# Two-layer streaming encoder trunk on one core: token tiles in another order, layer-norm scale and bias applied at the transposed copy, pooling loads ahead of the reloads, all gate units in the attention filler

## The chip, the cores and the metric

The kernel runs on one core of one Trainium2 chip. The metric is the device time of one execution in microseconds (us). The kernel before takes 2465.11 us, the median of three runs (2463.23 to 2467.07).

## What is computed

Two request groups, 1024 prompt tokens and 8 x 16 sample tokens, go through the same two layers of width 1024. The kernel treats them as T = 1152 tokens in nine tiles of 128; tile 8 is the sample group. The reference, cut to what matters:

```python
x = layer_norm(x, ln_in_g, ln_in_b)                      # entry
for each layer:
    h = x @ w_in -> px | pg | q | k | v | ag | ga | gb   # 512 | 512 | 5 x 1024 | 1024
    ya = pool_mix(px, history)  * silu(pg)               # 4 channel groups, windows 2, 4, 8, 16, each times w_pool[g]
    q, k = rope(q), rope(k)
    o  = diff_attend(q, k, v)                            # A1 - lambda * A2, RMS sub-norm per head
    yb = o * silu(ag)
    merged = sigmoid(ga) * (ya @ w_a) + sigmoid(gb) * (yb @ w_b)
    x = layer_norm(ALPHA * x + merged @ w_o, ln_g, ln_b)
```

All is fp32. Outputs are x of both groups and, for each layer, k, v and the last 15 rows of px.

## The kernel before

**Products.** A matrix product is made of three float32r products of a high and a low part: `xh` is a rounded copy of x (ScalarE), `xl` the rest (VectorE), and the same for weights (`wh`, `wl`, or `fa`, `fb` for some pieces). x is kept transposed, channels on partitions, for all nine token tiles.

**Weights.** Class `Weights` (L156 to L276) walks a fixed plan. `load` issues the DMA of the next piece into one of two staging tiles `ws`; `fill` splits staged pieces into hi (ScalarE, L243 or L257) and lo (VectorE, L244 or L258) as far as buffers are free; `get` hands a piece to its user and `free` gives its buffer back and fills again. For paired pieces `add` makes the four sums s1 to s4 (L195 to L198).

**Queues.** All DMAs are issued by SyncE (SP), in the order of the program. A DMA that waits (for its source to be written, or for its destination to be free) holds every DMA behind it. `later(n, fn)` puts an action off by n calls of `tick()`.

**Stages of a layer:**

1. *Entry (first layer) and first half of v.* A token tile's layer norm is statistics on VectorE (L374), `rs` and `nm` on GpSimd (L321, L326), two activations of 128x512 on ScalarE (L330), then gamma on VectorE (L335) and beta on GpSimd (L336). `to_T` (L300) transposes the finished tile on TensorE, copies it out of PSUM once as `xh` (L309) and once as fp32 `xs` (L312), with `xl` in between on VectorE (L310), and stores `xs` to the DRAM tensor `xT_d` (L313). The loop at L506 runs the nine tiles of v (`v_tile`, 24 matmuls of 128x512, L296 to L298); after each comes one step of `entry_rest` (L418): affine of one tile, norm of the next, transposition of an earlier one. gamma and beta are spread to 128 partitions by matmuls with a row of ones (L389). In the second layer the norm and affine steps belong to the end of the first, and only three transpositions remain for the loop.
2. *Operands of the seven-product scheme.* The rest of `x @ w_in` that is done at this point (q, k, px, pg, and ga) is computed in 16 pairs of 256 columns by a Strassen-like scheme: seven products e1 to e7 for each half c of the columns within the two token halves. The token half is HT = 576, a half of it CW = 288. For each c, `x_loads` reads four blocks of `xT_d` into `f` tiles (L471), `x_sums` makes t1 to t4 of them on VectorE (L477 to L480, 128x1152 each), and `x_split` makes hi and lo (L488, L489). t1 is written over a quadrant of `xh` and `xl`, which is saved in `b12_d` before (L513) and read back after the stage (L704). Products e1 and e2 use x itself and are the only ones that don't need t1 to t4. In the loop at L506 the loads for c = 0 come after tile 5 (first layer) or 3, those for c = 1 after tile 7 or 5, fixed in `l0, s0, l1, s1`.
3. *Lead.* In the first layer one attention-gate unit (72 matmuls, L528 to L541) stands between v and the products; LEAD = (1, 0).
4. *Products.* L555 to L698: the list `order` holds the products of all pairs, with the last product e7 of a column half held back by one; each result is joined on VectorE (L632) and leaves through rotation, tanh or a copy. After each finished operand `W.fill` is put off by one tick.
5. *Second half of v, with pooling.* L700 to L815. After the `b12_d` reload and small constants, the generator `pooling` loads two groups of px (`u_load`, L756 to L758), the gate values `sg` (L763) and the group's weights `wpl` (L765). It makes the window sums (`win_sums`), stores the history (`o_hp`, `o_hs`, L781 and L782) and forms the difference `pl` (`pool_diff`). `pool_mm` (L742) multiplies by `wpl` in three products of 128x384 (six rows of the trace), and writes `yah` and `yal`. One step of it follows each v tile: sums of group 0, product of group 0, sums of group 1, product of group 1, and so on. The loads of the next `sg` and `wpl` follow each product. `u` has two buffers: the loads of group 2 wait for the `o_hs` store of group 0.
6. *w_a*, then *attention* with two fillers: `filler` puts gate units (L882 and on) and w_b between the attention's matmuls, so that TensorE has work while softmax runs elsewhere. Then *w_o* with the layer norm (L1395 to L1470).

Of the kernel before, what the change touches and what calls it, by code (L numbers as in the profile page):

```python
# [17 lines left out]
P = 128  # L18
# [13 lines left out]
LEAD = (1, 0)  # L32
# [11 lines left out]

STEPS = [(1, 3), (2, 1), (4, 2), (3, 2), (3, 3), (1, 3, 4), (3, 5), (5, 5), (3, 5)]
# [11 lines left out]
def trunk(ctx, tc, a):  # L57
# [51 lines left out]
    cfix = const.tile([P, 4, 16], F32, name="cfix")  # L109

# [44 lines left out]
    class Weights:  # L155


        OPS = ("a11", "a12", "s1", "s2", "s4", "s3", "a22")

        def __init__(self):  # L160
# [13 lines left out]
            self.sums = None  # L174
            self.added = -1

        def load(self):
            while self.nload < len(self.loads) and self.held < NS:
# [8 lines left out]
                if e[0] == "p" and len(self.staged[i]) == 2 and self.sums is not None:  # L187
                    later(4, lambda i=i: self.add(i))

        def add(self, i):  # L190
            if self.added >= i:
                return
            self.added = i
            e1, e2 = self.staged[i]
            (sa, sb) = self.sums  # L195
            a11, a12, a21, a22 = e1[:, :512], e1[:, 512:], e2[:, :512], e2[:, 512:]
            s1, s2, s3, s4 = sa[:, :512], sa[:, 512:], sb[:, :512], sb[:, 512:]
            V.tensor_tensor(out=s1, in0=a21, in1=a22, op=ALU.add)  # L198
            V.tensor_tensor(out=s2, in0=s1, in1=a11, op=ALU.subtract)
            V.tensor_tensor(out=s4, in0=a12, in1=s2, op=ALU.subtract)  # L200
            V.tensor_tensor(out=s3, in0=a11, in1=a21, op=ALU.subtract)
# [18 lines left out]
        def fill(self, upto=1 << 30):  # L220
            while self.nsplit < min(len(self.items), upto):
                i, op = self.items[self.nsplit]
                tags = self.tags(op)
                if tags is None or (op is not None and op[0] == "s" and self.sums is None):
                    break
# [3 lines left out]
                if op is None:  # L229
# [8 lines left out]
                    else:  # L238
                        o = 4 * int(tags[0][1])
                        hi, lo = (x[:, o:o + 4, 2 * GW:2 * GW + 256] for x in (xh, xl))  # L240
# [5 lines left out]
                else:  # L246
                    if op[0] == "s":
                        self.add(i)
# [51 lines left out]
    def to_T(xn, t, pool, dst, one=None):  # L300
        two = None if one else ps_two()
        for b in range(2):
            ps = one() if one else two[:, b, :]
# [54 lines left out]
    gt = ep.tile([P, D], F32, name="gt")  # L358
    bt = ep.tile([P, D], F32, name="bt")
    dma(gt[0:1, :], a["ln_in_g"])  # L360
    dma(bt[0:1, :], a["ln_in_b"])
    for t in range(3):
        e_load(t)
    ones = ep.tile([1, P], F32, name="ones")
    G.memset(ones, 1.0)
    W.load()
    for t in range(3, 6):
        e_load(t)
# [15 lines left out]
    def spread(dst):  # L384
        out = []
        for b in range(2):
            ps = ps_any()
            c = slice(b * 512, (b + 1) * 512)
            PE.matmul(ps, ones, dst[0:1, c], start=True, stop=True)  # L389
            out.append((dst[:, c], ps))  # L390
        return out

    gps, bps = spread(gt), spread(bt)
    for dst, ps in gps:
        S.copy(dst, ps)
    e_norm(0)
    for dst, ps in bps:
        S.copy(dst, ps)
    e_norm(1)
    e_affine(0)  # L400
    e_norm(2)
    e_affine(1)
    e_turn(0)
    tick()
    e_affine(2)
    W.fill(1)
    W.fill(2)
    W.load()
    e_turn(1)
# [4 lines left out]
    e_turn(2)  # L414
    tick()
    for t in range(6, NT):
        e_load(t)

    def entry_rest():
        for n in range(3, NT + 2):  # L420
            if 3 <= n - 1 < NT:
                e_affine(n - 1)
# [1172 lines left out]
```

## Time and profile before

| what | value |
|---|---|
| median of three runs | 2465.11 us |
| profiled execution | 2470.53 us |
| its span | 2468.8 us |
| mean granted TensorE clock | 0.98 |
| TensorE busy | 2329.7 us, 94% |
| VectorE, ScalarE, GpSimd busy | 61%, 38%, 21% |

The stages lie as follows in the profiled execution, by the first matmul of each: first half of v from 25.4 us, lead unit from 98.4, products from 118.5, second half of v with pooling from 448.7, w_a from 519, attention from 575.7, w_o from 1153.8; second layer: v from 1257.0, products from 1316.0, pooling from 1646.8, w_a from 1721, attention from 1777.2, w_o from 2360.7.

To read it: a granted clock of 1.00 is TensorE at full speed, 0.50 at half. In a row of the waits, an engine's idle time is put down to what ended it. TensorE's rows have modelled ends, and matmuls overlap, so the time of one is not its pitch; the pitch is the difference of two starts.

### The profile page before, as it was taken

The page shows a single profiled execution, that of the slowest core. Times are in us where ns is not written, and L with a number is a line of the kernel's source. Part 1 is how long each engine was busy: PE and PEld are TensorE (multiplying, and loading weights), DVE is VectorE, ACT ScalarE, POOL GpSimd, SP SyncE. Part 2 cuts the span into 40 slices and gives each one's busy share as a digit, 9 for nine tenths or more (in the row PEclk, how much of TensorE's full clock was granted, in tenths as well). Part 3 has the DMA queues.
Part 4 walks back from the last instruction along what each step waited for, and adds up shares of the span by engine and source line. Part 5 has one row for each costly group of instructions (what it writes and reads, how often), then busy time and mean ns, then how long its engine had stood idle before and what let it go on. Part 6 is the DMA issues. An engine that isn't in the chain of part 4 may idle for free.

```text
span 2468.8 us, 40176 instructions
## 1 busy us (share of the span) xinstructions
PE 2329.7 (94%) x14936; PEld 2171.4 (88%) x14936; DVE 1510.9 (61%) x2903; ACT 932.7 (38%) x2054; POOL 519.0 (21%) x426
## 2 busy tenths in 40 slices
PE   7799999898999999999997999989899999999998
PEld 5689999687899998899877999987889898999986
DVE  5488854445677667744637886535467667666355
ACT  4332233212555555521433223332155555554122
POOL 4123300000121212232320332000012122213333
PEclk9999999899999999999998999999999999999999
DMA  6733323655555545365345233344745454545632
GB/s 213 240 109 102 98 103 102 172 162 179 158 163 151 155 136 156 111 215 192 128 158 161 94 100 111 103 150 117 233 139 170 120 176 125 171 132 167 207 131 77
DMA packets 241288, 363.42 MB, mean 147 GB/s; under 512 B 49218, under 2 KB 185410, under 8 KB 241092
## 3 DMA queue, kind: packets, MB, share of 16 engines
q1 hardware_dynamic: 241092, 360.85, 47.3%
q8 instruction: 118, 1.93, 0.3%
q14 instruction: 78, 0.64, 0.1%
HBM read 248.13 MB, written 112.62 MB: 146 GB/s over the span
## 4 chain that ended last, share of the span: by engine, by line
PE 71%; DMA 9%; DVE 9%; ACT 4%; issue 3%; SPq 2%; POOL 1%; ACTq 0%; DVEq 0%; POOLq 0%
PE ps_lin L282 6%; PE ps_lin L283 6%; PE ps_lin L284 6%; PE ps_tr L1062 4%; PE ps_lin L573 4%; PE ps_lin L571 4%; PE ps_lin L572 4%; PE ps_tr L1047 2%; PE ps_tr L571 2%; PE ps_tr L573 2%; PE ps_tr L572 2%; PE ps_lin L296 2%; PE ps_lin L297 2%; PE ps_lin L298 2%; PE ps_two L1016 2%
## 5 line engine op out<-in xcount | busy, mean ns | idle before, releaser
L282 PE MATMUL ps_lin<-xh,wh 128*128 128x384 f32 x1048 | 368.3, 351 | 0.9 <-ACT xh L1176 0.9
L284 PE MATMUL ps_lin<-xh,wl 128*128 128x384 f32 x1048 | 354.1, 338 | 0.0
L283 PE MATMUL ps_lin<-xl,wh 128*128 128x384 f32 x1048 | 353.7, 338 | 0.3 <-DVE xl L1177 0.3
L282 PEld LDWEIGHTS ps_lin<-xh,wh 128*128 128x128 f32 x1048 | 198.7, 190 | 6.3 <-issue 3.2
L283 PEld LDWEIGHTS ps_lin<-xl,wh 128*128 128x128 f32 x1048 | 198.8, 190 | 2.4 <-DVE xl L1177 0.8
L284 PEld LDWEIGHTS ps_lin<-xh,wl 128*128 128x128 f32 x1048 | 198.0, 189 | 0.0
L244 POOL TENSOR_TENSOR wl<-ws,wh 128x1024 fp32r<-128x1024 f32 x33 | 81.4, 2466 | 420.3 <-ACT wh L243 414.5
L1024 ACT ACTIVATE p<-ps_two,anm 128x640 f32<-128x640 f32 (+3 forms) x128 | 122.4, 956 | 103.1 <-DVE anm L1022 90.9
L1062 PE MATMUL ps_tr<-vt,at 128*128 128x128 f32 x1152 | 151.5, 277 | 4.5 <-ACT at L1049 4.4
L1062 PEld LDWEIGHTS ps_tr<-vt,at 128*128 128x128 f32 x1152 | 145.0, 192 | 9.4 <-ACT at L1049 9.2
L609 POOL TENSOR_TENSOR tt<-tt 128x288 f32<-128x288 f32 x64 | 62.3, 973 | 350.2 <-DVE tt L608 262.7
L1022 DVE TENSOR_REDUCE anm<-ps_two 128x1 f32<-128x640 f32 (+3 forms) x128 | 131.2, 1025 | 4.4
L1006 ACT ACTIVATE p<-ps_two,anm 128x128 f32<-128x128 f32 (+3 forms) x128 | 66.4, 524 | 168.4 <-DVE anm L1002 146.6
L243 ACT CAST wh<-ws 128x1024 fp32r<-128x1024 f32 (+1 forms) x74 | 73.9, 1003 | 115.8 <-PE ps_lin L283 52.1
L1036 DVE SCALAR_TENSOR_TENSOR p<-p,acc 128x128 f32<-128x128 f32 (+7 forms) x128 | 110.6, 864 | 4.5
L1047 PE MATMUL ps_tr<-ident,p 128*128 128x128 f32 x576 | 86.3, 276 | 21.8 <-DVE r L1037 13.7
L1049 ACT COPY at<-ps_tr 128x512 f32<-128x512 f32 (+1 forms) x192 | 86.4, 484 | 50.4 <-PE ps_tr L1047 49.7
L852 POOL TENSOR_TENSOR kl<-fx,kh 128x1024 fp32r<-128x1024 f32 x16 | 40.8, 2550 | 300.8 <-DMA fx<-q_d 165.5
L1047 PEld LDWEIGHTS ps_tr<-ident,p 128*128 128x128 f32 x576 | 68.7, 142 | 33.4 <-issue 9.9
L1016 PE MATMUL ps_two<-kh,qs 128*128 128x320 f32 (+3 forms) x256 | 94.6, 373 | 1.2 <-ACT p L1006 1.2
L1054 DVE COPY osb<-ps_tr 128x128 f32<-128x128 f32 x144 | 41.5, 288 | 82.5 <-PE ps_tr L1062 80.9
L1017 PE MATMUL ps_two<-kl,qs 128*128 128x320 f32 (+3 forms) x256 | 89.0, 351 | 0.0
(539 smaller groups left out, 6896.6 us busy)
## 6 DMA issues: line engine op xcount, KB each, us to landing
ws<-wt SPq DMA_DIRECT2D x96, 512.0 KB, 4.1
mt_d<-th SPq DMA_DIRECT2D x96, 192.0 KB, 3.8
fx<-q_d SPq DMA_DIRECT2D x128, 128.0 KB, 4.7
fx<-o_k SPq DMA_DIRECT2D x128, 128.0 KB, 4.1
st<-ck SPq DMA_DIRECT2D x32, 512.0 KB, 5.3
fx<-cv SPq DMA_DIRECT2D x32, 512.0 KB, 4.3
mt<-mt_d SPq DMA_DIRECT2D x42, 384.0 KB, 4.5
xT_d<-xs SPq DMA_DIRECT2D x36, 256.0 KB, 2.6
```

The lines of the kernel that those rows point to most:

```text
L282: PE.matmul(ps, wh[:, k, :], xh[:, k, :], start=(k == 0), stop=False),
L283: PE.matmul(ps, wh[:, k, :], xl[:, k, :], start=False, stop=False),
L284: PE.matmul(ps, wl[:, k, :], xh[:, k, :], start=False, stop=(k == nk - 1)))
L571: PE.matmul(ps, wh[:, k, :], oh[:, k, :], start=first and k == 0, stop=False, **more)
L572: PE.matmul(ps, wh[:, k, :], ol[:, k, :], start=False, stop=False, **more)
L573: PE.matmul(ps, wl[:, k, :], oh[:, k, :], start=False, stop=k == 3, **more)
L1016: PE.matmul(s[:, b, :c], qs[:, ql], kh[:, kc], start=True, stop=False)
L1022: V.tensor_reduce(out=nm[:, m:m + 1], in_=s[:, :, :c], axis=AX.XY, op=ALU.max, negate=True)
L1024: S.activation(out=p[:, :n].rearrange("p (b c) -> p b c", b=2), in_=s[:, :, :c], func=AF.Exp, bias=nm[:, m:m + 1], accum_out=ls_[:, m:m + 1])
L1036: V.scalar_tensor_tensor(out=pt[0], in0=pt[1], scalar=cc, in1=pt[0], op0=ALU.mult, op1=ALU.add)
L1047: PE.transpose(tr[:, j * P:(j + 1) * P], p[:, (b0 + j) * P:(b0 + j + 1) * P], ident)
L1062: PE.matmul(o_ps, hd["at", i][b // 4][:, (b % 4) * P:(b % 4 + 1) * P], hd["vt", b // 4][:, b % 4, :], start=(b == 0), stop=(b == i))
```

## The change

- The token tiles are taken in the order `TO` = 4, 5, 6, 0, 1, 2, 7, 8, 3 in the entry, in the first half of v and in w_o.
- `to_T` now transposes the normed tile before gamma and beta. It applies them as scale and bias of the copy out of PSUM: eight activations of 128x128 (one for each 128 channels, with columns of the new constant `lncol`), then hi and lo from the SBUF tile `xs`. gamma and beta on the natural layout (for the residual `x_d`) follow, in the entry as four GpSimd operations a tile, in the layers as VectorE multiply and GpSimd add. The `x_d` store of the entry is put off by two ticks. The matmuls that spread gamma and beta are replaced by broadcast DMAs.
- The table `X_STEPS` places saves ("b"), loads ("l"), sums ("s") and splits ("x", t1 too) for each half c in the loop of v, the first half's loads after the fifth v tile of the first layer and after the third of the second. Saves cover one half c each.
- The sums s1, s2 and s3, s4 of a weight pair are made apart, and the operand order is s2, s1, s3, s4; the products run e1, e2, e4, e3, e6, e5, e7. After the last three products of the stage `W.fill` isn't called.
- In the pooling stage the loads of `u`, `sg` and `wpl` stand ahead of the small constants and of the `b12_d` reload. The sums run one group ahead of the products by the table `steps`, and `W.fill` is called after the sixth v tile. `pl` has two buffers. `yal` is computed after the loop.
- LEAD is (0, 0): the first layer's lead unit goes to the attention filler.

GpSimd in the entry, before: one `x<-x,bt` pair for each tile, and each tile's `rs` and `nm` (the layer norm's scale and shift) between them.

```order
L336 TENSOR_TENSOR x<-x,bt 128x512 x2
L321 TENSOR_TENSOR rs<-ve,mhalf 128x1
L326 TENSOR_SCALAR nm<-mv,rs 128x1
L336 TENSOR_TENSOR x<-x,bt 128x512 x4
L321 TENSOR_TENSOR rs<-ve,mhalf 128x1
L326 TENSOR_SCALAR nm<-mv,rs 128x1
L336 TENSOR_TENSOR x<-x,bt 128x512 x2
```

The same place now:

```order
L349 TENSOR_TENSOR x<-x,gt 128x512
L350 TENSOR_TENSOR x<-x,bt 128x512
L349 TENSOR_TENSOR x<-x,gt 128x512
L350 TENSOR_TENSOR x<-x,bt 128x512
L335 TENSOR_TENSOR rs<-ve,mhalf 128x1
L340 TENSOR_SCALAR nm<-mv,rs 128x1
L349 TENSOR_TENSOR x<-x,gt 128x512
```

The third tile's `rs` stands behind the four affine operations of the first tile, which need the broadcast gamma and beta.

SP in the first layer's v loop, before, around the loads of half c = 0 (`f`, the blocks of `xT_d`; `ws` a weight, `b_d` the saved quadrant, `o_v` the v output):

```order
L461 DMA o_v<-vsb 128x512
L471 DMA f_650<-xT_d_86 128x4x288
L471 DMA f_652<-xT_d_86 128x4x288
L471 DMA f_654<-xT_d_86 128x4x288
L471 DMA f_656<-xT_d_86 128x4x288
L183 DMA ws<-wt 128x1024
L313 DMA xT_d_86<-xs 512x1x128 x2
L382 DMA x_d_84<-x 128x1024
L461 DMA o_v<-vsb 128x512
```

And now:

```order
L451 DMA o_v<-vsb 128x512
L485 DMA b_d_299<-xh 512x1x288
L485 DMA b_d_299<-xl 512x1x288
L461 DMA f_656<-xT_d_87 128x4x288
L461 DMA f_658<-xT_d_87 128x4x288
L461 DMA f_660<-xT_d_87 128x4x288
L461 DMA f_662<-xT_d_87 128x4x288
L393 DMA x_d_85<-x 128x1024
L327 DMA xT_d_87<-xs 512x1x128 x2
L451 DMA o_v<-vsb 128x512
```

Two more `xT_d` stores follow these loads in both; the saves now precede them, and an `x_d` store, which waits for GpSimd's affine, stands between them and the next `xT_d` store.

SP in the first layer's pooling stage, before, from the first `sg` and `wpl` to the second:

```order
L763 DMA sg<-sg_d_293 128x1152
L765 DMA wpl<-wpool 128x128
L183 DMA ws<-wa 128x512 x2
L461 DMA o_v<-vsb 128x512
L781 DMA o_hp<-u 128x15
L782 DMA o_hs<-u 1024x1x15
L756 DMA u<-px_d_292 128x1024
L757 DMA u<-px_d_292 128x8x16
L758 DMA u<-state 128x8x15
L461 DMA o_v<-vsb 128x512
L763 DMA sg<-sg_d_293 128x1152
L765 DMA wpl<-wpool 128x128
```

And now, up to the second `sg` and `wpl`, from the `u` loads of group 2 on:

```order
L721 DMA u<-px_d_297 128x8x16
L722 DMA u<-state 128x8x15
L190 DMA ws<-wa 128x512
L451 DMA o_v<-vsb 128x512
L745 DMA o_hp<-u 128x15
L746 DMA o_hs<-u 1024x1x15
L720 DMA u<-px_d_297 128x1024
L721 DMA u<-px_d_297 128x8x16
L722 DMA u<-state 128x8x15
L451 DMA o_v<-vsb 128x512
L727 DMA sg<-sg_d_298 128x1152
L729 DMA wpl<-wpool 128x128
```

Between the first `wpl` and the second there are now two stores of history and two reloads of `u`, of groups 2 and 3, where there was one of each.

The diff, cut to its core:

```diff
-LEAD = (1, 0)
+LEAD = (0, 0)
+TO = (4, 5, 6, 0, 1, 2, 7, 8, 3)
...
+X_STEPS = (
+    {4: (("b", 0), ("l", 0)), 5: (("s", 0), ("x", 0, "t1")), 6: (("b", 1), ("l", 1), ("x", 0, "t2", "t3", "t4")),
+     7: (("s", 1), ("x", 1, "t1")), 8: (("x", 1, "t2", "t3", "t4"),)},
+    {2: (("b", 0), ("l", 0)), 4: (("s", 0), ("x", 0, "t1", "t2", "t3", "t4"), ("b", 1), ("l", 1)),
+     6: (("s", 1),), 7: (("x", 1, "t1", "t2", "t3", "t4"),)})
...
-        OPS = ("a11", "a12", "s1", "s2", "s4", "s3", "a22")
+        OPS = ("a11", "a12", "s2", "s1", "s3", "s4", "a22")
...
-    def to_T(xn, t, pool, dst, one=None):
-        two = None if one else ps_two()
+    def to_T(xn, t, pool, dst, one, gb):
...
-            src = ps.rearrange("p (j t) -> p j t", j=4)
-            S.copy(hi, src)
-            V.tensor_tensor(out=lo, in0=src, in1=hi.bitcast(F32), op=ALU.subtract)
             xs = pool.tile([P, 4, P], F32, tag="xs", name="xs", bufs=2)
-            S.copy(xs, src)
+            for j in range(4):
+                k = 4 * b + j
+                S.activation(out=xs[:, j], in_=ps[:, j * P:(j + 1) * P], func=AF.Identity,
+                             bias=lncol[:, gb, 1, k:k + 1], scale=lncol[:, gb, 0, k:k + 1])
+            S.copy(hi, xs)
+            V.tensor_tensor(out=lo, in0=xs, in1=hi.bitcast(F32), op=ALU.subtract)
...
-    def e_affine(t):
-        ln_affine(e_x[t], gt, bt, (V, V), None)
-
     def e_turn(t):
-        to_T(e_x[t], t, ep, xT_d[0], ps_any)
-        later(1, lambda: dma(x_d[0][t * P:(t + 1) * P, :], e_x[t]))
+        to_T(e_x[t], t, ep, xT_d[0], ps_any, 0)
+        ln_affine(e_x[t], gt, bt, (G, G))
+        later(2, lambda: dma(x_d[0][t * P:(t + 1) * P, :], e_x[t]))
...
-        for t in range(NT):
+        for n, t in enumerate(TO):
             v_tile(t, 0, pieces, vs_half())
...
+            for step in X_STEPS[l].get(n, ()):
+                f, c, names = {"l": x_loads, "s": x_sums, "b": b12_save, "x": x_split}[step[0]], step[1], step[2:]
+                f(c, *names)
...
-            return [e1, e2, e3, e4, e5, e6, e7]
+            return [e1, e2, e4, e3, e6, e5, e7]
...
             if done:
                 W.free(1, fill=False)
-                later(1, W.fill)
+                if n < len(order) - 3:
+                    later(1, W.fill)
...
-        for x, d in ((xh, b12_d[0]), (xl, b12_d[1])):
-            dma(x[:, 0:4, HT:].bitcast(F32), d)
...
+        us_[0] = u_load(0)
+        if l == 0:
+            dma(cfix, a["cfix"])
+        us_[1] = u_load(1)
+        gi[0] = g_in(0)
...
+        for x, d in ((xh, b12_d[0]), (xl, b12_d[1])):
+            dma(x[:, 0:4, HT:].bitcast(F32), d)
+        pool_sum(0)
+        steps = {0: (pool_sum, 1), 1: (pool_out, 0), 2: (pool_sum, 2), 3: (pool_out, 1), 4: (pool_sum, 3),
+                 5: (pool_out, 2), 7: (pool_out, 3)}
...
             v_tile(t, 1, pieces, vs_half())
             tick()
-            next(pooled, None)
...
+            if t in steps:
+                steps[t][0](steps[t][1])
+            if t == 5:
+                W.fill()
```

More of the change, by code (lines that the diff above doesn't have):

```diff
@@ L109, in trunk @@
     cfix = const.tile([P, 4, 16], F32, name="cfix")
+    lncol = const.tile([P, 2, 2, KD], F32, name="lncol")
     xh = xp.tile([P, KD, T], F32R, name="xh")
@@ L173, in __init__ @@
             self.spare = 1
-            self.sums = None
-            self.added = -1
+            self.sums = ()
+            self.added = set()
         def load(self):
@@ L223, in fill @@
                 tags = self.tags(op)
-                if tags is None or (op is not None and op[0] == "s" and self.sums is None):
+                if tags is None or (op is not None and op[0] == "s" and len(self.sums) <= (int(op[1]) - 1) // 2):
                     break
@@ L356, in e_load @@
             dma(e_x[t], a["x_prompt"][t * P:(t + 1) * P, :] if t < SEQ // P else a["x_sample"])
[L358 to L362, printed above, removed]
+    dma(lncol, a["lncol"])
+    for t in TO[:2]:
         e_load(t)
-    ones = ep.tile([1, P], F32, name="ones")
-    G.memset(ones, 1.0)
     W.load()
-    for t in range(3, 6):
+    for t in TO[2:5]:
+        e_load(t)
+    gt = bcast(ep, a["ln_in_g"], "gt")
+    bt = bcast(ep, a["ln_in_b"], "bt")
+    for t in TO[5:]:
         e_load(t)
@@ L375, in e_norm @@
         ln_norm(x, *ln_scale(st))
-    def e_affine(t):
-        ln_affine(e_x[t], gt, bt, (V, V), None)
     def e_turn(t):
-        to_T(e_x[t], t, ep, xT_d[0], ps_any)
-        later(1, lambda: dma(x_d[0][t * P:(t + 1) * P, :], e_x[t]))
[L384 to L403, printed above, removed]
+        to_T(e_x[t], t, ep, xT_d[0], ps_any, 0)
+        ln_affine(e_x[t], gt, bt, (G, G))
+        later(2, lambda: dma(x_d[0][t * P:(t + 1) * P, :], e_x[t]))
+    for n in range(2):
+        e_norm(TO[n])
+    W.fill(1)
+    e_turn(TO[0])
     tick()
-    e_affine(2)
-    W.fill(1)
+    e_norm(TO[2])
     W.fill(2)
     W.load()
-    e_turn(1)
+    e_turn(TO[1])
     tick()
@@ L687, in trunk @@
         order.append(held)
-        for f, need, done in order:
+        for n, (f, need, done) in enumerate(order):
             if need:
@@ L749, in pool_mm @@
                 S.copy(yah[:, pg, c], sg[:, c])
+            for g in range(NG):
+                c = slice(g * GW, (g + 1) * GW)
                 V.tensor_tensor(out=yal[:, pg, c], in0=sg[:, c], in1=yah[:, pg, c].bitcast(F32), op=ALU.subtract)
@@ L782, in pool_diff @@
             dma(a["o_hs"][l, pg * P:(pg + 1) * P], us[:, :, DS:])
-            pl = ap.tile([P, T], F32, tag="pl", name="pl")
+            pl = ap.tile([P, T], F32, tag="pl", name="pl", bufs=2)
             V.tensor_tensor(out=cur[:, HIST:HIST + win - 1], in0=cur[:, HIST:HIST + win - 1],
@@ L1413, in trunk @@
         bt = bcast(cp, a["ln_b"][l], "bt")
-        for t in range(3):
+        for t in TO[:3]:
             z_load(t)
@@ L1441, in trunk @@
         pieces = [W.get()[1] for _ in range(8)]
-        for t in range(NT):
+        at_ = lambda n: TO[n] if n < NT else None
+        for n, t in enumerate(TO):
             for u in range(2):
@@ L1486, in trunk @@
             bc_ctx.close()
-            estep = (t_step(t) for t in range(6, NT))
+            estep = (t_step(t) for t in TO[6:])
 def _layout(inp):
```

212 lines of the change are left out of this document (93 added, 119 removed).

## The prediction

> **What bounds the kernel now.** I read the page first, then the span by stretches, then what TensorE waited for, then the chain that ended last.
>
> ```profile
> span 2468.8 us, 40176 instructions
> PE 2329.7 (94%) x14936; PEld 2171.4 (88%) x14936; DVE 1510.9 (61%) x2903; ACT 932.7 (38%) x2054; POOL 519.0 (21%) x426
> ```
>
> TensorE is the bound, and the change takes no matmul of weight from it. All that can be won is in its 139 us of idle time and in stretches at half clock. The stretches (columns: length, then busy time of PE, PEld, DVE, ACT, POOL, then the granted clock) show where those lie:
>
> ```profile
> 95.00:135.00 40.00, 28.15 (x130) 25.08 (x129) 28.64 (x29) 14.53 (x21) 0.00 (x0) 0.81 0.61 210
> 440.00:520.00 80.00, 67.23 (x284) 53.24 (x283) 42.04 (x60) 17.82 (x32) 0.39 (x4) 0.91 0.58 156
> 1260.00:1345.00 85.00, 68.54 (x343) 58.54 (x342) 41.88 (x51) 27.63 (x44) 8.61 (x8) 0.90 0.54 176
> 1640.00:1723.00 83.00, 69.36 (x296) 54.81 (x296) 42.47 (x61) 17.80 (x33) 0.38 (x4) 0.92 0.57 152
> ```
>
> These are the way into the first layer's products, its pooling stage, and the same two places of the second layer. TensorE's waits name what ended the idle time (total, times, longest):
>
> ```profile
> PE ps_lin L746 <- DMA wpl<-wpool: 13.1, 2, 10.1
> PE ps_tr L571 <- ACT wh L257: 10.2, 1, 10.2
> PE ps_tr L746 <- DMA wpl<-wpool: 9.4, 1, 9.4
> PE ps_lin L571 <- DVE vsb L538: 7.4, 1, 7.4
> PE ps_lin L571 <- DVE tt L632: 7.3, 4, 3.0
> ```
>
> Pooling waits for its weights' DMA, the products wait at their beginning for operands, and four times for a join. The chain of the first 135 us, in order of time, tells why the products begin late (start, length, what):
>
> ```profile
> 11.31 1.26 POOL x L336
> ...
> 60.97 2.27 POOL x L336 x2
> 70.03 2.27 POOL x L336 x2
> ...
> 86.28 7.78 DMA xT_d<-xs
> ...
> 106.31 7.43 DMA f<-xT_d
> ...
> 115.22 1.37 DVE f L479
> ...
> 127.26 1.27 DVE t2l L489
> ...
> 131.06 1.28 DVE xl L489
> ...
> 466.21 3.84 DMA wpl<-wpool
> ```
>
> Steps of the entry are 70.03 - 60.97 = 9.06 us apart and go through GpSimd's beta; then come a store of `xT_d`, the second loads of `f`, the sums and splits of c = 1 (L479, L489), and a last split that ends at 132.34.
>
> **The change part by part.** *Entry.* What a step needs on each engine:
>
> ```profile
> 83.42 0.39 PE L296 MATMUL ps_tr<-wh,xh 128*128 128x512 f32 x1
> 85.93 0.39 PE L298 MATMUL ps_tr<-fa,xl 128*128 128x512 f32 x1
> L330 ACT ACTIVATE z<-z,nm,rs 128x512 f32<-128x512 f32 x34 | 25.8, 807 | 42.3 <-POOL nm L326 42.3
> L1049 ACT COPY at<-ps_tr 128x512 f32<-128x512 f32 x96 | 54.8, 588 | 46.5 <-PE ps_tr L1047 45.8
> L1056 ACT ACTIVATE jk<-ps_tr 128x128 bf16<-128x128 f32 x144 | 40.2, 279 | 52.3 <-DVE ar L1033 24.9 <-DVE osb L1054 19.6 <-DVE wv__23115 L1138 3.6
> L336 POOL TENSOR_TENSOR x<-x,bt 128x512 f32<-128x512 f32 x18 | 26.6, 1494 | 27.6 <-DVE x L335 27.2 <-ACT bt L398 0.4
> L321 POOL TENSOR_TENSOR rs<-ve,mhalf 128x1 f32<-128x1 f32 x9 | 5.4, 600 | 17.9 <-DVE ve L319 17.9
> ```
>
> Eleven matmuls lie between the first two rows' starts, 2.51 us: 0.228 each, so a v tile's 24 take 5.5, and with its eight transpositions (at most the same pitch, 1.8; I take 1) TensorE needs 6.5. ScalarE now has one v copy (0.59), two norm halves (1.61), two hi copies (1.18) and eight copies of 128x128 with pointer scale and bias. No row shows such a copy; without pointers one takes 0.279, and with them 128x512 takes 0.807 against 0.588, 0.22 more. That makes 0.50 each, eight 4.0, and a step 7.4 on ScalarE. GpSimd has four affine halves and a norm: 4 x 1.494 + 0.6 + about 0.3 = 6.9. beta is no longer ahead of the transposition, so the step goes from 9.06 to ScalarE's 7.4, 1.7 less.
>
> When are the loads of c = 0 issued? The SP rows of before:
>
> ```profile
> 81.18 3.31 SPq L471 DMA_DIRECT2D f<-xT_d  x4
> 104.24 3.91 SPq L471 DMA_DIRECT2D f<-xT_d  x4
> 95.85 1.35 DVE L477 TENSOR_TENSOR f<-f,f 128x1152 f32<-128x1152 f32 x1
> 101.30 1.35 DVE L489 TENSOR_TENSOR t2l<-f,t2h 128x1152 fp32r<-128x1152 f32 x1
> ```
>
> They are issued after the sixth v tile now and after the fifth then: one step (9.1) plus four shorter ones (6.8) earlier, about 2 more because the first v tile no longer waits for spread matmuls, less about 1 for the `x_d` store, which waits for GpSimd's affine and stands ahead on SP: 17 us, at about 64. Sums (from 95.85 on) and splits of c = 0 move along, 17 earlier, to about 79 to 90; the second loads wait for those buffers, as now, and go from 104.24 to about 87; they land by 95. Sums (four of 1.36) and three or four splits (1.3 each) then end at 106, with weight sums at 107.5 to 110. Before, 9.3 us lay between the end of the sums of c = 1 (115.22 + 1.37, and one more of 1.36) and their first split there at 127.26, about 7 of them VectorE's weight fills and sums; most of these now fit into the wait for the loads. So the fourth product starts 22 to 25 us earlier (17 and up to 7); I take 22. The cover of the wait, the lead unit, is gone from here, so TensorE idles longer before the fourth product, which is in that figure.
>
> The lead's matmuls reappear in the attention. The second layer's attention shows the price, having one gate unit more:
>
> ```profile
> 575.70:1153.80 578.10, 555.93 (x3793) 526.01 (x3793) 368.87 (x817) 265.81 (x663) 132.99 (x85) 0.99 0.53 156
> 1777.15:2360.70 583.55, 567.36 (x3866) 539.00 (x3865) 369.31 (x820) 268.94 (x667) 133.89 (x86) 0.99 0.52 157
> ```
>
> It has 11.4 us more of TensorE and lasts 5.45 longer. I charge 5.5, at most 11.4. The way into the first products is worth 22 - 5.5 = **16.5**, between 9 and 24.
>
> *Order of the products.* The join waits (7.3 in both layers) come where e7 follows e6's long join; with e5 between them and no fills at the end I count all **7.3**, at least 3.
>
> *First pooling stage.* The first matmul of the stage, and SP's rows of before:
>
> ```profile
> 448.73 0.63 PE L296 MATMUL ps_tr<-wh,xh 128*128 128x512 f32 x1
> ...
> 457.33 0.33 SPq L756 DMA_DIRECT2D u<-px_d  x1
> ...
> 466.21 0.43 SPq L765 DMA_DIRECT2D wpl<-wpool  x1
> 469.11 0.61 SPq L782 DMA_DIRECT2D o_hs<-u  x1
> 475.65 0.33 SPq L756 DMA_DIRECT2D u<-px_d  x1
> ```
>
> The `wpl` load is issued 8.9 us after the first `u`, and lands at 466.21 + 3.84 = 470.05. Now the eight issues between are pure issue time, about 4.3; but the skipped fills leave all four v weight pieces to be cast when the products end, two of them only after the first two's buffers and loads, so I put the first v tile 5 us later, and the `ws<-wa` loads ahead of `u` wait for those casts: `u` at 10.5 after the stage's begin (448.7) instead of 8.6, `wpl` landed at 19 instead of 21.3. That is 2 won. The second output then waits longer: its `sg` and `wpl` stand behind `u` of groups 2 and 3, each of which waits for an `o_hs` store, and 475.65 - 469.11 = 6.5 is what such a wait takes. Counted from the stage's begin, sums of group 0 end at about 20, `u` of group 2 is issued at 27, `o_hs` of group 1 at 28.5, `u` of group 3 at 35, `wpl` at 38, landed at 42. TensorE would be there at 35: a new gap of 7 to 8. After a gap it runs cold:
>
> ```profile
> 1667.75:1672.80 5.05, 5.00 (x9) 3.02 (x10) 2.18 (x5) 1.02 (x2) 0.00 (x0) 0.50 0.50 134
> ```
>
> This stretch follows the second layer's gap of 10.1: 5 us at 0.50, 2.5 lost. New gap 7.5 and 2.5 of cold clock, less 2 won, and part of the later first tile hidden in the old gap: I take **-6**, between -12 and +8 (if SP isn't held, the 9.4 and its cold clock go). The Trainium skill ("TensorE: Matmul & The Clock Gate", Part 1: The HAM clock gate) has full clock return after one busy window of about 3.4 us; by it the cold clock would cost 1.7 instead of 2.5, and the stage -5.
>
> *Second pooling stage.* Here the first pieces are cast before the stage begins, `u` goes out at once, and the 10.1 goes to about 1 or 2; the second output's chain runs as above, some 6 us earlier, and takes most of it back: **-0.5**, between -9 and +9.
>
> *Way into the second layer's products.* The wait of 10.2 ends with a split of c = 1 operands and a sum of weights. Beta no longer stands on GpSimd ahead of the last tiles' transpositions, and c = 1 is loaded one to two tiles earlier; the loads of c = 0 now wait for affine stores. I take **4**, 0 to 8.
>
> Sum: 16.5 + 7.3 - 6 - 0.5 + 4 = 21.3. The profiled execution took 2470.5, 5.4 above the median of 2465.1; it would be 2449.2, and the median 2443.8.
>
> **The rivals.** *SP isn't held in the pooling stages.* If `u` and `wpl` come as the order was laid out, both stages lose their wait: 13.1 + 9.4 and half of two cold stretches of 5 us, 27.5, in place of my -6.5. With the other terms (16.5 + 7.3 + 4 = 28) that is 55 at most; with half of the 27.5 given back by later outputs' waits it is 41, so 2424. For it: the loads are ahead of 2.4 MB of reload. Against it: `ws<-wa` still stands before them.
>
> *GpSimd becomes the entry's bound.* Its 6.9 a step is near 7.4, and one row of the same operation is longer than the 1.26 of the first:
>
> ```profile
> 19.15 3.85 POOL L336 TENSOR_TENSOR x<-x,bt 128x512 f32<-128x512 f32 x2 [2.80 <-DVE x L335]
> ```
>
> At 1.9 a half a step would be 8.5, and the norm of the next tile and the `x_d` store ahead of the loads would wait: 1.1 x 4 steps and some 3 for the store, twice over for the second loads, 9 to 10 less: 2453. The Trainium skill ("GPSIMD Engine Reference", Specifications) says that GpSimd shares its SBUF interfaces with VectorE and is in contention with VectorE instructions of two SBUF inputs; the low part `xl` now reads two of them, where it read PSUM and SBUF.
>
> *Slower: the pooling chain on SP.* If each later output, not only the second, waits for a round of `o_hs` (6.5), `u` (1.5) and `sg`, `wpl` (4), it is 12 us a round, against 5.5 x 2 of v tiles and 2 to 3 of products between outputs, so a wait only appears where rounds pile up two deep, as they do for the second output. With the DMAs of the `b12_d` reload still in flight and `o_hs` waits of 10 rather than 6.5, two rounds last 31 where TensorE has some 15 of its own work: a gap of 16 and 3 of cold clock, 19 in each layer. That is 38 lost against 28 won elsewhere, 2475. It decides from a round of about 14 us on (two are 28, less 15, with 3 of cold clock 16, in both layers 32).
>
> *Off the path.* If the fourth product still waits for the last `xT_d` tile, or the lead costs its full 11.4 and joins still wait, some 15 are left less 10: 2460 to 2465.
>
> **How the numbers follow.** A measurement of this kernel can tell about 0.2% (4.9 us) from no change. My forecast, with gains of 12 to 32, has 0.55; SP not held 0.18; GpSimd's bound 0.13; off the path 0.06; slower 0.08. The likeliest is 2444. The unknown costs reach from +9 + 3 - 12 - 9 + 0 = -9 to 24 + 9 + 8 + 9 + 8 = 58, but not all at one end: the range is 2420 to 2463, which leaves out the slower case, part of the one off the path, and the best of SP not held. Faster by over 0.2%: 0.55 + 0.18 + 0.13 = 0.86; within it: 0.06; slower: 0.08.
>
> **What would show it.** Right: steps of the first v loop 7 to 7.5 apart with ScalarE busy all through; c = 0 loads at about 64 and the fourth product complete at about 112; no wait for a join over 1 us; an attention 5 to 6 longer in the first layer; one wait of TensorE for `wpl` in each pooling stage, at the second output. Wrong: `u` issued within 5 us of the first pooling stage's begin; steps of 8.5; two or more waits of over 10 in a pooling stage.

## The result, and the profile after

The changed kernel is slower: 2507.33 us (median of four runs, 2503.51 to 2511.24) against 2464.56 us; the ratio is 1.0172, with a 95% interval of 1.0154 to 1.0191. The prediction was 2444, in a range of 2420 to 2463. The profiled execution took 2503.5 us, 33.0 more than that of before, and is the fastest of its four runs; the stages below account for these 33. The medians differ by 42.8: the profiled execution of before lies 6.0 above its median, and this one 3.8 below.

The page's first lines, and TensorE's waits (total, times, longest):

```profile
span 2501.7 us, 40201 instructions
...
PE 2327.2 (93%) x14928; PEld 2174.5 (87%) x14928; DVE 1488.5 (59%) x2884; ACT 965.9 (39%) x2158; POOL 548.6 (22%) x444
```

```profile
PE ps_tr L708 <- DMA wpl<-wpool: 22.4, 2, 16.7
PE ps_lin L542 <- ACT sb L599: 20.4, 6, 14.0
PE ps_lin L708 <- DMA wpl<-wpool: 19.3, 2, 16.1
PE ps_tr L318 <- ACT x L344: 18.5, 2, 9.5
PE ps_two L1054 <- DMA st<-ck: 11.9, 2, 6.1
```

TensorE's busy time, 2327.2, has hardly changed (2329.7 before), so the loss is idle time: 174.5 us against 139.1. The weights `wpl` of the pooling stage cost 41.7 us of waiting where they cost 22.5; the products wait 14.0 ahead of the third of them; a wait for `st` at the beginning of the attention has doubled. By stages, from the first matmul of one to that of the next (the attention from the first matmul of its own, at 579.2 in the kernel before, and the last w_o to its last matmul):

| stage | before | after | difference |
|---|---|---|---|
| to the first product | 118.5 | 103.5 | -15.0 |
| products, first layer | 330.2 | 341.7 | +11.5 |
| pooling and v, first layer | 70.4 | 88.3 | +17.9 |
| w_a | 60.0 | 60.3 | +0.3 |
| attention | 574.5 | 579.6 | +5.2 |
| w_o, and v of the second layer | 162.4 | 161.9 | -0.5 |
| products, second layer | 330.6 | 332.7 | +2.0 |
| pooling and v | 74.6 | 83.9 | +9.3 |
| w_a | 60.0 | 59.8 | -0.1 |
| attention | 579.4 | 582.0 | +2.6 |
| w_o | 98.1 | 98.1 | 0.0 |

The first two rows belong together: the lead unit (12.7 us) is gone from the first, but the third product starts at 125.1 against 126.6, so that TensorE waits instead. A product is 12 matmuls; the 217th matmul, the first of the 19th product, has all the waits at the beginning behind it. It starts at 158.1 against 160.9, and the attention pays for the unit.

**Pooling.** SP's rows of the first layer's stage, which begins at 445.18, and the row of TensorE that waits:

```profile
466.79 0.63 SPq L783 DMA_DIRECT2D xl<-b_d  x1
...
468.13 0.69 SPq L746 DMA_DIRECT2D o_hs<-u  x1
479.45 0.33 SPq L720 DMA_DIRECT2D u<-px_d  x1
...
484.14 0.59 SPq L746 DMA_DIRECT2D o_hs<-u  x1
490.06 0.33 SPq L720 DMA_DIRECT2D u<-px_d  x1
...
493.85 0.44 SPq L729 DMA_DIRECT2D wpl<-wpool  x1
```

```profile
498.56 1.62 PE L708 MATMUL ps_tr<-pl,wpl 128*128 128x384 f32 x2 [16.73 <-DMA wpl<-wpool]
```

Two reloads of `u` wait, one after the other, for a history store to land: 479.45 - 468.13 = 11.3 for the first, behind the reload of the saved quadrant, 5.9 for the second. The second `sg` and `wpl`, whose buffers were free at about 474 (the end of the first output's last low part on VectorE), are issued only then. The clock follows (length, busy times, then the granted clock; TensorE's busy time is the first):

```profile
445.18:533.49 88.31, 64.74 (x241) 48.72 (x242) 40.70 (x58) 14.66 (x25) 0.22 (x2) 0.85 0.52 137
1667.93:1751.82 83.89, 61.90 (x243) 46.99 (x241) 38.46 (x56) 14.07 (x25) 0.22 (x2) 0.86 0.54 139
```

**Entry.** One step, on ScalarE, then VectorE, GpSimd, and ScalarE again:

```profile
59.14 1.52 ACT L344 ACTIVATE x<-x,nm,rs 128x512 f32<-128x512 f32 x2 [2.96 <-POOL nm L340]
60.57 1.48 ACT L323 ACTIVATE xs<-ps_lin,lncol 128x128 f32<-128x128 f32 x4
62.08 0.62 ACT L325 CAST xh<-xs 128x512 fp32r<-128x512 f32 x1
62.61 1.50 ACT L323 ACTIVATE xs<-ps_tr,lncol 128x128 f32<-128x128 f32 x4
64.14 0.62 ACT L325 CAST xh<-xs 128x512 fp32r<-128x512 f32 x1
...
68.21 1.52 ACT L344 ACTIVATE x<-x,nm,rs 128x512 f32<-128x512 f32 x2 [2.96 <-POOL nm L340]
```

```profile
64.79 0.69 DVE L326 TENSOR_TENSOR xl<-xs,xh 128x512 fp32r<-128x512 f32 x1 [1.29 <-ACT xh L325]
```

```profile
67.26 0.55 POOL L335 TENSOR_TENSOR rs<-ve,mhalf 128x1 f32<-128x1 f32 x1 [2.62 <-DVE ve L333]
```

The step is 68.21 - 59.14 = 9.07 us, as before. No engine is full: of the 9.07 us TensorE is busy for 7.5 (at a granted clock of 0.83), GpSimd for 6.2 and ScalarE for 6.0. The round sets it: norm, eight copies and two hi parts on ScalarE, the last low part and then the next tile's statistics on VectorE, `rs` and `nm` on GpSimd, and back to the norm.

### The profile page after: what moved, and what is told of

Read it like the earlier page. It is cut to its first block, busy times and chain, and to the rows that moved or that the text cites. A ratio compares the mean times of both kernels' runs of the same rounds, so it can differ in the third digit from the quotient of the medians.

```text
span 2501.7 us, 40201 instructions
## 1 busy us (share of the span) xinstructions
PE 2327.2 (93%) x14928; PEld 2174.5 (87%) x14928; DVE 1488.5 (59%) x2884; ACT 965.9 (39%) x2158; POOL 548.6 (22%) x444
## 5 line engine op out<-in xcount | busy, mean ns | idle before, releaser
L293 PE MATMUL ps_lin<-xh,wh 128*128 128x384 f32 x1072 | 376.0, 351 | 0.9 <-ACT xh L1155 0.9
L294 PE MATMUL ps_lin<-xl,wh 128*128 128x384 f32 x1072 | 361.8, 338 | 0.3 <-DVE xl L1156 0.3
L295 PE MATMUL ps_lin<-xh,wl 128*128 128x384 f32 x1072 | 361.7, 337 | 0.0
L255 POOL TENSOR_TENSOR wl<-ws,wh 128x1024 fp32r<-128x1024 f32 x34 | 83.9, 2467 | 416.7 <-ACT wh L254 405.2
L1003 ACT ACTIVATE p<-ps_two,anm 128x640 f32<-128x640 f32 (+3 forms) x128 | 122.3, 956 | 97.7 <-DVE anm L1001 94.3
L1026 PEld LDWEIGHTS ps_tr<-ident,p 128*128 128x128 f32 x576 | 68.6, 141 | 28.3 <-DVE ysb L1132 7.0
```

The lines of the kernel that those rows point to most:

```text
L255: self.lo_engine.tensor_tensor(out=lo, in0=st, in1=hi.bitcast(F32), op=ALU.subtract)
L293: PE.matmul(ps, wh[:, k, :], xh[:, k, :], start=(k == 0), stop=False),
L294: PE.matmul(ps, wh[:, k, :], xl[:, k, :], start=False, stop=False),
L295: PE.matmul(ps, wl[:, k, :], xh[:, k, :], start=False, stop=(k == nk - 1)))
L1003: S.activation(out=p[:, :n].rearrange("p (b c) -> p b c", b=2), in_=s[:, :, :c], func=AF.Exp, bias=nm[:, m:m + 1], accum_out=ls_[:, m:m + 1])
L1026: PE.transpose(tr[:, j * P:(j + 1) * P], p[:, (b0 + j) * P:(b0 + j + 1) * P], ident)
```

## The experiments

Theory A: in the pooling stage the second `sg` and `wpl` stand on SP behind reloads of `u` that wait for history stores. Theory B: the DMA engines are busy with the reload. Theory C: the entry's step is a round across engines; theory D: one engine holds it.

**u_copy.** The history goes out from a copy that ScalarE makes:

```diff
-            dma(a["o_hs"][l, pg * P:(pg + 1) * P], us[:, :, DS:])
...
+            S.copy(hs, us[:, :, DS:])
...
+            dma(a["o_hs"][l, pg * P:(pg + 1) * P], hs)
```

> The changed kernel, with the history rows copied to a small tile by ScalarE and stored from there, so that the reload of u for groups 2 and 3 no longer waits for a history store; order of the queue as in the changed kernel. Theory A (in the pooling stage the second sg and wpl stand on SP behind two reloads of u that wait for the history stores): the reloads go out as soon as the sums are done, the second wpl is issued about 474 us instead of 493.9 in the first layer, TensorE's waits for it of 16.7 and 16.1 us go to under 2, and with the cold clock behind them the pooling stages go from 88.3 and 83.9 us to about 70 and 68; in all 30 to 37 us faster than the changed kernel, about 2472. Theory B (the loads are late because the DMA engines are busy with the reload of the saved quadrant): the waits stay within 3 us of what they are, 2505.

Measured: 2484.71 us, ratio to before 1.0084 (1.0064 to 1.0105); stages of 76.7 and 73.9. The 16 us waits are 6.7 and 6.9. The stages win back 21.6 us of the profile's 27.2, so A holds much of it. But `wpl` was issued at 483.9 and not at 474, since the third `u` and a weight stood in the queue for 2.1 and 4.7 us, and that is not in A. Nor does the edit take away the waits alone: the copy's rows lie together, and the run has 236660 DMA packets where the changed kernel has 243828.

**u_behind.** Only the queue's order:

```diff
-            if pg < 2:
-                us_[pg + 2] = u_load(pg + 2)
+            if pg == 2:
+                us_[3] = u_load(3)
...
                 gi[pg + 1] = g_in(pg + 1)
+            if pg == 0:
+                us_[2] = u_load(2)
```

> The changed kernel, with only the order of the queue altered: the reload of u for group 2 goes behind the second sg and wpl, that for group 3 behind the sums of group 2. History stores still hold the reloads. Theory A: the second wpl is issued at about 475 us in the first layer, the waits of 16 us go to under 3, but the sums of group 2 start later and the third output may wait 0 to 5; 25 to 35 us faster than the changed kernel, about 2477. Theory B (busy DMA engines): no change, 2505.

Measured: 2490.78 us, 1.0100 (1.0085 to 1.0115); stages of 80.1 and 74.7. SP's row, TensorE's row, and the stretch between (the number behind the clock of 0.74 is the DMA engines' busy share, twice that of the stages above):

```profile
476.01 0.44 SPq L729 DMA_DIRECT2D wpl<-wpool  x1
```

```profile
488.62 1.62 PE L708 MATMUL ps_tr<-pl,wpl 128*128 128x384 f32 x2 [9.13 <-DMA wpl<-wpool]
```

```profile
476.00:488.50 12.50, 3.49 (x16) 2.56 (x14) 0.00 (x0) 1.17 (x2) 0.22 (x2) 0.74 1.14 119
```

It was issued when A said, and landed 12.5 us later, where the first `wpl` of the stage took 3.4. So A and B each hold a part.

**reload_late.** u_behind, with the reload put behind the second `wpl` and the third `u`:

```diff
             if pg == 0:
                 us_[2] = u_load(2)
+                for x, d in ((xh, b12_d[0]), (xl, b12_d[1])):
+                    dma(x[:, 0:4, HT:].bitcast(F32), d)
...
-        for x, d in ((xh, b12_d[0]), (xl, b12_d[1])):
-            dma(x[:, 0:4, HT:].bitcast(F32), d)
```

> The changed kernel with the order of u_behind and the reload of the saved quadrant put behind the second sg, wpl and the third u. In u_behind the second wpl was issued at 476.0 us, as theory A said, but landed 12.5 us later, behind the 2.4 MB of reload: so both theories hold a part. With the reload out of the way: the second wpl lands within 5 us of its issue, TensorE's waits for wpl at the second output go from 16.7 and 16.1 us to under 2 in both layers, the fifth v tile may wait up to 4 us for the reload; pooling stages of 68 to 73 us, the kernel 2470 to 2478. If waits on history stores alone were the cause: no better than u_copy, 2485.

Measured: 2489.14 us, 1.0075 (1.0053 to 1.0098); stages of 79.4 and 74.0, no better than u_behind, where 68 to 73 was expected. TensorE's rows:

```profile
481.64 1.25 PE L708 MATMUL ps_tr<-pl,wpl 128*128 128x384 f32 x2 [2.08 <-DMA wpl<-wpool]
...
487.95 0.47 PE L307 MATMUL ps_lin<-wh,xh 128*128 128x512 f32 x1 [2.49 <-DMA xh<-b_d]
...
492.06 0.80 PE L309 MATMUL ps_lin<-wh,xl 128*128 128x512 f32 x1 [3.40 <-DMA xl<-b_d]
```

The wait for `wpl` went as expected (it landed 7.7 us after its issue), and came back as a wait of the fifth v tile for the quadrant, 5.9 us and longer than the 4 expected. Put early, the reload stands ahead of loads that TensorE waits for; put late, TensorE waits for it. In its old place ahead of all, the kernel before waits for `wpl` 9.4 us in the first layer, at the first output, and 10.1 and 3.0 in the second.

**old_pool.** The pooling stage and the fills as before, all else changed.

> The changed kernel with one part undone: the pooling stage (order of loads, sums and products, constants, reload first) as before, and W.fill called after every product as before. If the pooling stage's new order holds the loss: its stages go from 88.3 and 83.9 us to 70 to 77 and 72 to 75, the attention's wait for st from 6 to 3 in both layers, and the kernel is 26 to 34 us faster than the changed one, 2470 to 2480. What is left above the kernel before would be the lead unit (5) and the second layer's operands (1 to 2). If the loss were spread over the rest of the change: less than 15 faster.

Measured: 2480.84 us, 1.0046 (1.0031 to 1.0060); the profiled execution is 24.4 us below the changed kernel's. Stages of 80.8 (70 to 77 was expected) and 71.5, waits for `st` of 3.2 and 2.4. The pooling stage's new order therefore holds most of the loss. The second layer's stage is better than before's 74.6; the first layer's lacks 10 us, because its first v tile ends 11.5 us after the begin and not 6.5, and the first output comes at 28.3, not 21.5.

**fills_on.** `W.fill` after the last three products too.

```diff
-                if n < len(order) - 3:
-                    later(1, W.fill)
+                later(1, W.fill)
```

> The changed kernel with W.fill called after the last three products too. The changed kernel's first v tile of the first pooling stage ends 13.0 us after the stage's begin, before 6.5. If the skipped fills do that: it ends at 6 to 9, u goes out earlier, and the first output comes at 15 to 20 instead of 21.9; but the second output is set by the chain on SP and comes at 45 to 53 instead of 53.4. So 0 to 8 us faster than the changed kernel. If the later first tile were of no matter: no change.

Measured: 2504.32 us, 1.0140 (1.0124 to 1.0157). The first v tile ends at 11.4 instead of 13.0, so the fills are the smaller part of it; the second output comes at 52.7, set by SP as expected.

**stats_ahead.** The next tile's statistics before the previous tile's low part:

```diff
...
             if n < NT:
                 e_norm(TO[n])
+            if n + 1 < NT:
+                e_stats(TO[n + 1])
```

> The changed kernel, with the statistics, rs and nm of a token tile made one step ahead of its norm in the entry, before the previous transposition's low part on VectorE. Theory C (the entry's step of 9.06 us is one round of norm and copies on ScalarE, low part and statistics on VectorE, rs and nm on GpSimd, back to ScalarE): the step falls to the busiest engine's 6.5 to 7.0, the first loads of f are issued at about 65 us instead of 76, the products' 217th matmul comes 8 to 12 us earlier (158.1 before), and the kernel is 7 to 12 us faster than the changed one. Theory D (ScalarE with its eight pointer copies, or GpSimd with four affine halves, holds the step): the step stays at 9.

Measured: 2504.40 us, 1.0157 (1.0138 to 1.0177). Transpositions of TensorE, two steps:

```profile
55.10 0.60 PE L318 MATMUL ps_lin<-ident,x 128*128 128x128 f32 x4
...
61.45 0.60 PE L318 MATMUL ps_tr<-ident,x 128*128 128x128 f32 x4
```

The step is 6.35 us, and now an engine is full: TensorE is busy for all of it, ScalarE for 6.05. C holds, D falls. But the loads of `f` come at 70.3 instead of 76.0, the 217th product matmul only 4.3 earlier, and the total gains nothing clear. The next wait is ScalarE's, for the last tile's copy:

```profile
85.33 1.51 ACT L323 ACTIVATE xs<-ps_tr,lncol 128x128 f32<-128x128 f32 x4 [10.40 <-DMA xT_d<-xs]
```

**xs_four.** stats_ahead, with four `xs` buffers in the entry instead of two.

> The kernel of stats_ahead with four instead of two fp32 copies xs of a transposed tile in the entry. There ScalarE waits 10.4 us for a store of xT_d that stands behind the loads of f, before it can copy the last tile, and the sums of c = 0 stand behind that tile's low part on VectorE. If that store is what holds the sums: the last tile's copies start at about 75 us instead of 85.3, the sums of c = 0 at about 81 instead of 90.2, and the products' 217th matmul comes 6 to 9 us earlier than stats_ahead's 153.8; 6 to 9 faster than stats_ahead. If the f loads or the weights set it: the same matmul within 2 us.

Measured: 2498.76 us, 1.0113 (1.0088 to 1.0138). The last tile's copies start at 75.5, the sums at 81.2, and the 217th matmul at 146.3, 7.6 earlier than in stats_ahead. The products end 9 us earlier, and the second output of the pooling stage waits 22.9 instead of 20.1.

**lq_behind.** `lq` allocated behind `yah` and `yal`.

> The changed kernel with the tile lq allocated behind yah and yal instead of ahead of them. In the changed kernel lq is the first tile of the pooling pool and takes the buffers th with it to the place where the attention's cmask lies later, so that cmask's load, and st behind it on SP, waits for the last mt_d stores: TensorE waits 6.1 and 5.8 us for st where it waited 3.3 and 2.4. Expected: st's waits back to about 3 and 2.5, the kernel 5 to 7 us faster than the changed one. If st is late for another reason: no change.

In the changed kernel SP's load of `cmask`, which the loads of `st` follow, waits 4 us:

```profile
1810.32 0.34 SPq L868 DMA_DIRECT2D mt_d<-th  x1
1814.49 0.33 SPq L880 DMA_DIRECT2D cmask<-cmask  x1
...
1818.46 0.91 SPq L941 DMA_DIRECT2D st<-ck  x2
```

With the tile moved, TensorE's waits for `st`:

```profile
PE ps_two L1054 <- DMA st<-ck: 5.5, 2, 3.1
```

These are 3.1 and 2.4 instead of 6.1 and 5.8, as expected: a reused address made the load wait. The attention stages are 1.0 and 3.3 us shorter, less than the waits. The total, 2503.34 us, 1.0133 (1.0104 to 1.0163), doesn't tell so little from the changed kernel's 1.0172 with its interval.

**old_no_lead.** The kernel before, with LEAD = (0, 0).

> The kernel before with LEAD = (0, 0) alone: the lead gate unit goes to the attention filler. If the operands of c = 1 set the start of the products whatever stands ahead of them: the 49th product matmul starts at most 5 us earlier than 136.1, the first attention gets 2 to 6 longer, and the kernel takes 2464 to 2468, no faster than before. If the lead stood on the path of the operands (its weight fills and joins on VectorE): the products start 8 to 12 earlier and the kernel is 4 to 8 faster.

Measured: 2470.68 us, 1.0018 (1.0009 to 1.0027): a little slower. The 217th matmul comes 4.6 earlier (156.25), with a wait of 17.1 us where the unit was; the first pooling stage takes 75.8 instead of 70.4 (its first v tile ends 8.5 after the begin, not 6.5), and the first attention 579.8 instead of 574.5, 5.3 more.

**old_order.** The kernel before, with the changed order of operands and products.

> The kernel before with the changed order of operands and products alone (e1, e2, e4, e3, e6, e5, e7, sums in two parts, rotation of the second half in e5). By the prediction the waits for joins go, 3 to 7 us faster than before. By the changed kernel's trace, where other waits of 3.2 us stand in their place at the first pair: within 3 us of before, with the first layer's way into the products a little shorter (two products that need no sum of four blocks come first no longer: e4 before e3).

Measured: 2475.19 us, 1.0017 (1.0004 to 1.0029). In the first layer the join waits of 1.9 and 3.0 are gone; waits of 3.7 and 3.3 for a join at the first pair came in their place, and the first v tile of the first pooling stage ends 8.6 us after its begin instead of 6.5. No gain.

**mix and mix_copy.** What these runs point to: xs_four, the third tile's statistics ahead of the first affine as well, and old_pool; mix_copy adds u_copy's copy.

> What the runs point to: the changed kernel with the pooling stage and fills as before (old_pool), statistics one step ahead, those of the third tile ahead of the first tile's affine, and four xs tiles (xs_four). The 217th product matmul comes at 143 to 147 us instead of 158.1 (160.9 before), the pooling stages and st waits as in old_pool; against the kernel before it wins 14 to 17 there, pays 5 for the lead unit in the attention and 1 to 3 in the second layer: 5 to 10 us faster than before, ratio 0.996 to 0.998. If a wait behind the products takes the gain back: no faster than before.

> The kernel mix with the history rows copied by ScalarE and stored from the copy, as in u_copy, so that reloads of u don't wait for the stores. In the old order of the pooling stage these waits stand off TensorE's path but for the third output of the second layer (3.0 us): 0 to 4 us faster than mix. If ScalarE's two copies a group delay the v copies: slower by up to 2.

Measured: mix 2464.40 us, 0.9976 (0.9965 to 0.9987); mix_copy 2460.47 us, 0.9960 (0.9947 to 0.9973). The 217th matmul comes at 142.5 and 142.7. In mix_copy TensorE still waits ahead of the third product, the longest of these, 13.8:

```profile
PE ps_lin L559 <- ACT sb L616: 20.8, 6, 13.8
```

**mix_lead and mix_lead_order.** mix_copy with the lead unit back (and t1 split behind it), then also with the old order of products.

> The kernel mix_copy with the lead gate unit back ahead of the products (LEAD = (1, 0), t1 split behind it, since t1 is written over what the unit reads). If the lead is worth its place: TensorE's wait of 13.8 us ahead of the fourth product shrinks to under 5, the 217th product matmul comes within 3 us of mix_copy's 142.7, the first attention is 5 us shorter, the first v tile of the first pooling stage ends at 9 to 10 instead of 12.1: 5 to 9 us faster than mix_copy. If the lead's weights and joins on VectorE delay the operands as they did before: the 217th matmul 6 to 10 later, no faster than mix_copy.

> mix_lead with the operands and products in the order of the kernel before. If the lead's move and the order of products make the first v tile of the first pooling stage late: it ends at 6 to 7 as before, and the first output comes at 21 to 23; against mix_lead 0 to 6 us faster in that stage, 2 slower at the last joins of the products, 2 to 4 faster at their beginning. If something else makes it late: the tile as in mix_lead.

Measured: mix_lead 2456.14 us, 0.9951 (0.9934 to 0.9968); mix_lead_order 2452.13 us, 0.9926 (0.9909 to 0.9943), the fastest of all: 17 us below the kernel before on the same chip. The unit fills the wait: 13.8 shrinks to 2.2, the 217th matmul is 3.9 later (at most 3 was expected), and the first attention 4.5 shorter. mix_lead's total is not told apart from mix_copy's: the intervals overlap. The first v tile of the first pooling stage ends at 8.4 and then 5.5 us after the begin, the first output at 25.0 and 22.8: the lead's move and the order of products made it late, as their single runs (8.5 and 8.6) had said. What TensorE waits for in mix_lead_order:

```profile
PE ps_tr L753 <- DMA wpl<-wpool: 11.7, 1, 11.7
PE ps_lin L753 <- DMA wpl<-wpool: 11.0, 1, 11.0
```

One wait for `wpl` a layer is left, at the first output.

## Why the prediction was wrong, by its own steps

The forecast for the profiled execution was 2449.2, and it took 2503.5. Of these 54 us, 19 lie in the way into the first products (16.5 forecast as won, 2.5 lost), 21 in the two pooling stages (6.5 forecast as lost, 27.2 lost), and 5 each in the order of the products and the second layer's way in.

- *Entry: "the step goes from 9.06 to ScalarE's 7.4".* This failed. The longest engine was taken for the step; the step is a round across three engines, and the change left it as long: the loads of c = 0 went out at 76.0, where 64 was forecast. The prices were near (a pointer copy 0.45 where 0.50 was worked out, ScalarE busy about 6.0 of the step). stats_ahead shows the bound of the busiest engine, TensorE: 6.35, where 6.5 was worked out. GpSimd, the bound in one rival, is busy for 6.2 of the 9.07.
- *"Sums (from 95.85 on) and splits of c = 0 move along".* This failed too. The sums did not hang on the loads of `f` alone: the last tile's copy waits for a store behind them on SP. It was on the chain that the prediction quoted (86.28), and xs_four shows it worth 7.6 us. The sums of c = 0 start at 95.44, where they started at 95.85. With both, the 16.5 became 2.8 earlier at the 217th matmul less the lead's 5.3, a loss of 2.5. The size was within reach: in mix the 217th comes 18.4 us before that of the kernel before.
- *"Most of these now fit into the wait for the loads"*, the 7 us of weight work on VectorE between the sums and the splits of c = 1. The splits did come earlier: the last of c = 1 ends at 122.3, before at 132.3. But the sums of the weights came hardly earlier, at 122.2 (123.9 before), since they now stand behind the splits; and TensorE's wait of 14.0 ended with a copy of ScalarE that stands behind the casts of these sums. VectorE's rows, then ScalarE's:

```profile
120.91 1.35 DVE L481 TENSOR_TENSOR t4l<-f,t4h 128x1152 fp32r<-128x1152 f32 x1
122.18 0.68 DVE L207 TENSOR_TENSOR sums<-ws 128x512 f32<-128x512 f32 x1
```

```profile
123.62 1.14 ACT L268 CAST wh<-sums 128x512 fp32r<-128x512 f32 x2 [4.53 <-DVE sums L208]
124.66 0.40 ACT L599 ACTIVATE sb<-ps_lin 128x288 f32<-128x288 f32 x1
```

So the 7 us reached the splits and not the products. This is read from the rows; no run moved the sums of the weights alone.
- *The lead, 5.5 in the attention.* Right: 5.3 in old_no_lead. That its place ahead of the products was the better one was not seen: old_no_lead is slower than the kernel before, and in mix_lead the wait that it fills shrinks from 13.8 to 2.2.
- *Order of products, 7.3.* Counting all join waits was wrong. From the 337th product matmul to the last one the first layer gains 2.2 and the second loses 0.2; at the first pair new waits of 3.2 came; old_order alone gains nothing.
- *Pooling, -6 and -0.5.* The place and the sign were right, the second output behind two reloads of `u`; the size was not: -17.9 and -9.3. The term that was mis-sized is the first history store, 6.5 from a row where the quadrant's reload had drained, and 11.3 now, since the reload was moved ahead of it. The second `wpl` was issued 48.7 after the stage's begin, where 38 was forecast. Of these 10.7 us the longer wait is 4.8; the store before it went out 2.4 later than the forecast's times imply (23.0, not 27 - 6.5 = 20.5), and 3.2 more lie between the first of these reloads of `u` and the next store, 4.7 where 1.5 was forecast. In the second layer the first output's wait went from 10.1 to 5.7 and not to 1 or 2, and the second output's, 16.1, took back more than all.
- *The rival on the slower side* had this mechanism, a gap of 16 and 19 us a layer, and was given 0.08: its condition, stores of 10 us behind the reload, could be expected from the order of the queue that was laid out, and should have had more weight. Its two rounds of 31 us were near: 30.3 from the first store's issue (468.13) to the landing of the second `wpl`. Only the first store took as long, though.
- *Cold clock.* A gap costs more than itself, as weighed: over the first pooling stage the granted clock was 0.85. By the records there it was 0.50 from 485.0 to 502.1, some 3.5 us beyond the 16.7 us gap (498.56), so 1.8 us lost. The rule of the Trainium skill ("TensorE: Matmul & The Clock Gate", Part 1: The HAM clock gate), at least one busy window of about 3.4 us, agrees: behind the second layer's gap of 16.1 it took 4.0, and behind the gaps of 9.4 and 10.1 in the kernel before 4.6 and 5.1.
- *Way into the second layer's products, 4.* It lost 1.4 (to the 337th matmul from the start of w_o): the loads of c = 1 still wait for the splits of c = 0, which end 156.9 after the start of w_o, before 158.1; the third product starts 176.8 after it, before 175.8.
- *Not seen at all:* the wait for `st`, 2.8 and 3.4 us longer, from a tile's address.

What stays open: whether the wait at the first pooling output (9.4 to 11.9 us in the kernels with the old stage) can be taken away without a later one. The changed kernel has 3.3 and 5.7 there and pays at the second output; no run moved the reload alone in the old stage, or made it smaller.

## What to carry to other kernels

The time of a pipelined step can be set by the longest round that comes back to its start, and not by the busiest engine: follow a tile's operations through the queue of every engine back to the same operation of the next tile before a cost is summed. A queue that is shared in order has no "ahead" for free: when a large transfer is moved behind small ones, look at which small ones now stand behind it, and at every wait that the reordered entries carry with them. A unit of work that seems movable may be the cover of a wait; price the place it leaves as well as the one that it goes to.

## What the runs showed of the hardware that was not expected

Operations of VectorE and GpSimd that run beside each other take longer. In xs_four the sums of c = 0 run beside GpSimd's last affine halves:

```profile
83.72 2.34 DVE L484 TENSOR_TENSOR f<-f,f 128x1152 f32<-128x1152 f32 x1
...
88.45 1.36 DVE L486 TENSOR_TENSOR f<-f,f 128x1152 f32<-128x1152 f32 x1
```

```profile
82.42 2.42 POOL L349 TENSOR_TENSOR x<-x,gt 128x512 f32<-128x512 f32 x1
```

The same operation takes 2.34 us beside GpSimd and 1.36 after it has ended, and GpSimd's half 2.42 where it takes 1.28 in the quiet part of the changed kernel's entry. In mix, mix_copy, mix_lead and mix_lead_order it is the same: 2.33 to 2.45 us for the three sums beside GpSimd, 1.36 for the fourth. (The third ends 1.2 us after GpSimd's last half by its row; GpSimd's spans are rough.) This is what the Trainium skill says ("GPSIMD Engine Reference", Specifications: the SBUF interfaces are shared, with contention for VectorE instructions of two SBUF inputs), with a size to it: some three quarters more for the one, and nearly double for the other. And in the changed kernel's first pooling stage a store of 60 KB took 11.2 us to land right behind the 2.4 MB of the reload, and the three later ones 5.3 to 7.6.
